# RMSNorm and SiLU on one core: transfers cut by partitions instead of by rows

## The chip, the core and the metric

The kernel runs on one core of one Trainium2 chip. The core has a buffer of 128 partitions, a vector engine (VectorE, DVE in the profile), an activation engine (ScalarE, ACT), a general engine (GpSimd, POOL), a matrix engine (TensorE, PE; here it does no arithmetic and only passes signals on), and a queue processor (SyncE, SP) that issues transfers. Sixteen DMA engines move data between the DRAM of the chip and the buffer. The metric is the device time of one execution in microseconds (us). The kernel before took 159.55 us as a median of three runs (159.41 to 160.32).

## The reference

The input `x` has 16 x 1024 rows of 512 float32 values. Each row is divided by its root mean square, multiplied by `gamma`, and put through the SiLU function:

```python
rms = np.sqrt(np.mean(x ** 2, axis=-1, keepdims=True) + eps)
x_norm = x / rms * gamma
return (x_norm * (1.0 / (1.0 + np.exp(-x_norm)))).astype(np.float32)
```

One row is 2 KB. All of `x` is 33.55 MB, the result as much, so 67.1 MB must pass through the DMA engines.

## The kernel before

**Tiles.** Every partition handles 128 rows (16,384 rows over 128 partitions). The buffer `xb` is a ring of 96 rows for each partition, 192 KB. Rows 0 to 95 of a partition have a place of their own in it; rows 96 to 127 go into the places of rows 0 to 31, once these are stored. All arithmetic is done in place, in units of `cn` = 4 rows (32 units).

**Rows in DRAM.** `groups` (L28) says which rows of DRAM belong to which rows of a partition. A group of g rows means that partition p owns g neighbouring rows of DRAM, so that a transfer of n of them is one unbroken piece of 2n KB for each partition. With groups of 16 a piece can be at most 32 KB, with groups of 32 it can be 64 KB. A piece of a partition is one packet of a DMA engine. A transfer over 128 partitions gives each of the sixteen engines eight packets.

**Transfers.** `loads` (L30 to L32) and `stores` (L33 to L35) list the transfers as (first row, rows); each covers all 128 partitions:

```python
    loads = [(0, 4), (4, 4), (8, 8), (16, 16), (32, 32), (64, 28), (92, 4)]
    loads += [(96, 16), (112, 12), (124, 4)]
    stores = [(0, 16), (16, 16)]
    stores += [(32, 32), (64, 32), (96, 16), (112, 8), (120, 8)]
```

`order` (L36 to L41) is the order by hand in which SP issues them, all on one queue: the seven loads of the first ring; a wait until load (64, 28) has landed; the two stores of rows 0 to 31 (the first middle phase); the three loads of rows 96 to 127 (the second middle phase); a wait until load (112, 12) has landed; the remaining stores. The first two loads are put ahead of the start barrier (`early`, L42). `load` (L127) lets SP wait for the stores whose places the load overwrites (L132): load (96, 16) waits for store (0, 16), load (112, 12) for store (16, 16). `store` (L138) waits until `s_swish` counts all units that hold its rows as done (L141). SP works in order: what waits holds up whatever stands behind it.

**Units.** For unit k, ACT squares the four rows (`square`, L205): two rows one by one with a sum (L207), two together into PSUM (L213); DVE sums the latter (`sums`, L232); POOL adds eps and takes the power -1/2 (`power`, L174); DVE multiplies each row by that and by gamma (`norm`, L241, L244); ACT applies SiLU (`swish`, L217, L219). ACT runs two units ahead with the squares (`lead`): after square k+2 comes swish k. Ten rounds of three units each run in a loop.

**Landings.** The first two squares wait for their loads themselves (L230). For all later units PE's queue waits for each load in turn (L168) and adds to `s_land` the number of units that are now complete; the square of a unit waits for that count.

## Time and profile before

| what | value |
|---|---|
| median of three runs | 159.55 us (159.41 to 160.32) |
| the profiled execution, its own time | 159.47 us |
| its span | 158.2 us |
| data moved | 67.12 MB, 424 GB/s over the span |
| ACT busy | 129.7 us (82%) |
| DVE busy | 124.5 us (79%) |
| POOL busy | 65.4 us (41%) |
| last SiLU ends | 143.8 us |

The span is the time between the first and the last instruction in the trace; the profiled execution's own time is 1.3 us longer. Busy times are sums over the whole span. The DMA rows of the page give the mean busy share of the sixteen engines; a queue's share is the time of its packets as a share of sixteen engines' span. The page lists no duration for a single packet, but the trace holds a record with start, duration and size for every packet; where such records are used they are called packet records.

### The profile page before, as it was taken

What the parts mean: (1) busy time and instruction counts of PE and PEld (TensorE: products, weight loads), DVE (VectorE), ACT (ScalarE), POOL (GpSimd) and SP (SyncE); (2) the same over time, 40 slices, a digit from 0 to 9 for tenths busy, and PEclk for the clock granted to TensorE, in tenths of its full rate; (3) what the DMA queues carried; (4) which work ended last, traced back from release to release, by engine and by line L of the source; (5) the groups of instructions that cost most, each with busy time, mean ns of one, the idle gap of its engine ahead of it and who ended that gap; (6) DMA issues with size and microseconds to landing.
All of it is one profiled execution on the core that took longest, in us unless ns stands there. A gap on an engine that the chain in (4) does not pass through costs nothing. (4 is left out here: it accounts for less than half of the span.)

```text
span 158.2 us, 696 instructions
## 1 busy us (share of the span) xinstructions
DVE 124.5 (79%) x162; ACT 129.7 (82%) x193; POOL 65.4 (41%) x70
## 2 busy tenths in 40 slices
DVE  0187968999199999999999999999999999980000
ACT  0949959996599999999999999999999999753000
POOL 1053555555055555555555555555555555510000
DMA  7999997979999879999999899996996998999896
GB/s 257 450 489 398 398 597 332 530 332 464 464 464 464 377 305 445 481 448 398 398 431 497 363 466 445 450 530 265 530 530 265 530 448 348 398 448 472 365 435 269
DMA packets 2456, 67.12 MB, mean 424 GB/s; under 512 B 276, under 2 KB 276, under 8 KB 280
## 3 DMA queue, kind: packets, MB, share of 16 engines
q1 hardware_dynamic: 2448, 67.11, 98.8%
q10 hardware_dynamic: 8, 0.01, 0.0%
HBM read 33.56 MB, written 33.55 MB: 424 GB/s over the span
## 5 line engine op out<-in xcount | busy, mean ns | idle before, releaser
L244 DVE SCALAR_TENSOR_TENSOR xb<-xb,rstd,gamma_sb 128x512 f32 (+1 forms) x128 | 87.3, 745 | 0.0
L219 ACT ACTIVATE xb<-xb (+1 forms) x32 | 60.9, 1903 | 2.8 <-DVE xb L244 2.8
L234 DVE TENSOR_REDUCE ms<-sq 128x2 f32<-128x1024 f32 x32 | 39.2, 1225 | 17.4 <-ACT sq L213 14.2
L177 POOL TENSOR_SCALAR aeps<-ms 128x4 f32<-128x4 f32 x32 | 20.6, 644 | 69.0 <-DVE ms L234 69.0
L184 POOL TENSOR_TENSOR rstd<-aeps,neg_half 128x4 f32<-128x4 f32 x32 | 44.1, 1378 | 2.7
L207 ACT ACTIVATE junk<-xb 128x512 f32 (+1 forms) x64 | 38.6, 603 | 7.8 <-PEq L168 7.5
L213 ACT ACTIVATE sq<-xb 128x1024 f32 (+1 forms) x32 | 32.2, 1005 | 0.0
L207 ACT ACTIVATION_READ_ACCUMULATOR junk<-xb 128x1 f32 x64 | 11.9, 186 | 0.0
L227 ACT ACT_TABLE_LOAD x1 | 1.3, 1283 | 3.6 <-issue 3.6
L170 POOL MEMSET gamma<- 128x512 f32 x1 | 0.5, 524 | 1.5 <-POOLq L75 1.5
L254 DVE STREAM_SHUFFLE gamma_sb<-gamma 128x512 f32<-128x512 f32 x1 | 0.7, 719 | 0.0
L319 POOL MEMSET const-float32-0.0<- 128x1 f32 x1 | 0.1, 98 | 0.2 <-issue 0.2
L171 POOL MEMSET neg_half<- 128x4 f32 x1 | 0.1, 102 | 0.0
L319 POOL MEMSET const-bfloat16-1.0<- 128x1 bf16 x1 | 0.1, 101 | 0.0
L319 POOL MEMSET const-uint8-127<- 128x1 uint8 x1 | 0.1, 101 | 0.0
L319 POOL MEMSET const-float32-1.0<- 128x1 f32 x1 | 0.1, 99 | 0.0
L254 DVE LOAD_MASK_SELECT gamma_sb<-gamma x1 | 0.0, 15 | 0.0
## 6 DMA issues: line engine op xcount, KB each, us to landing
out_dram<-xb SPq DMA_DIRECT2D x3, 4096.0 KB, 19.2
xb<-in_x_dram SPq DMA_DIRECT2D x2, 4096.0 KB, 19.5
xb<-in_x_dram SPq DMA_DIRECT2D x1, 7168.0 KB, 54.8
xb<-in_x_dram SPq DMA_DIRECT2D x4, 1024.0 KB, 12.9
out_dram<-xb SPq DMA_DIRECT2D x2, 2048.0 KB, 15.1
xb<-in_x_dram SPq DMA_DIRECT2D x1, 3072.0 KB, 16.8
xb<-in_x_dram SPq DMA_DIRECT2D x1, 2048.0 KB, 10.2
out_dram<-xb SPq DMA_DIRECT2D x2, 23.7
```

The costliest lines, as they stand in the source:

```text
L170: nc.gpsimd.memset(gamma4, 0.0).then_inc(s_zero, 1)
L171: nc.gpsimd.memset(neg_half, -0.5).then_inc(s_half, 1)
L177: nc.gpsimd.tensor_scalar(out=aeps[:, m, :], in0=ms[:, m, :], scalar1=eps_f, scalar2=None, op0=ALU.add,),
L184: nc.gpsimd.tensor_tensor(out=rstd[:, m, :], in0=aeps[:, m, :], in1=neg_half, op=ALU.pow),
L207: acc = nc.scalar.activation(out=junk[(k % turn) * (cn - n_sq) + j - n_sq], in_=rows(down(at, j), 1), func=AF.Square, scale=inv_d**0.5, ac ...
L213: nc.scalar.activation(out=sq[k % turn], in_=rows(at, n_sq), func=AF.Square, scale=inv_d**0.5,).then_inc(s_sq, 1)
L219: nc.scalar.activation(out=rows(at, cn), in_=rows(at, cn), func=AF.Silu),
L227: nc.scalar.preload_act_table_set("silu_and_others")
L234: nc.vector.tensor_reduce(out=ms[:, k % turn, 0:n_sq], in_=sq[k % turn], op=ALU.add, axis=mybir.AxisListType.X,),
L244: ins = nc.vector.scalar_tensor_tensor(out=one, in0=one, scalar=rstd[:, k % turn, j : j + 1], in1=gamma_sb, op0=ALU.mult, op1=ALU.mult,)
L254: nc.vector.stream_shuffle(gamma_sb, gamma4, [0] * 32), s_gld, 16
L319: nc = _bacc.Bacc("TRN2", target_bir_lowering=False, num_devices=1)
```

## The change

All groups have 32 rows. Each transfer has a third entry that says which partitions it covers: all (`every`), the even ones, the odd ones, or a part of the odd ones.

```diff
-    groups = [16, 16, 32, 32, 16, 16]
+    groups = [32, 32, 32, 32]
-    loads = [(0, 4), (4, 4), (8, 8), (16, 16), (32, 32), (64, 28), (92, 4)]
+    every, even, odd = (0, P), (0, P, 2), (1, P, 2)
+    loads = [
+        (0, 4, every),
+        (4, 12, every),
+        (16, 16, every),
+        (32, 32, every),
+        (64, 32, every),
+    ]
     second = len(loads)
-    loads += [(96, 16), (112, 12), (124, 4)]
-    stores = [(0, 16), (16, 16)]
+    loads += [
+        (96, 32, even),
+        (96, 32, (1, 128, 4)),
+        (96, 32, (3, 128, 8)),
+        (96, 32, (7, 128, 8)),
+    ]
+    stores = [(0, 32, even), (0, 32, odd)]
     storing = len(stores)
-    stores += [(32, 32), (64, 32), (96, 16), (112, 8), (120, 8)]
+    stores += [(32, 32, every), (64, 32, every), (96, 20, every), (116, 12, every)]
     order = [("load", i) for i in range(second)]
-    order += [("landed", loads.index((64, 28)))]
+    order += [("swished", 10)]
     order += [("store", t) for t in range(storing)]
     order += [("load", i) for i in range(second, len(loads))]
-    order += [("landed", loads.index((112, 12)))]
+    order += [("landed", 7)]
     order += [("store", t) for t in range(storing, len(stores))]
...
     def load(i):
-        a, n = loads[i]
-        for u, (c, m) in enumerate(stores):
+        a, n, p = loads[i]
+        for u, (c, m, q) in enumerate(stores):
             over = c + ring < a + n and a < c + m + ring
+            over = over and not set(range(*p)).isdisjoint(range(*q))
...
+        elif what == "swished":
+            nc.sync.wait_ge(s_swish, t)
...
+    passed = lead
+    for i in range(len(loads)):
+        landed = need(nc.tensor.nop(nofuse=True), ld[i], 16)
+        if landed_units[i] > passed:
+            landed.then_inc(s_land, landed_units[i] - passed)
+            passed = landed_units[i]
```

The even partitions of rows 0 to 31 are stored in one transfer of 64 partitions, the odd ones in a second. The even partitions of rows 96 to 127 are then loaded in one transfer (it waits for the even store), the odd ones in three: 32 partitions (1, 5, 9, ...), 16 partitions (3, 11, 19, ...) and 16 partitions (7, 15, 23, ...). The first of these three waits for the odd store. SP issues the first stores after ten units are through SiLU, where it waited for load (64, 28); it issues the later stores after the load of partitions 3, 11, ... has landed. A unit counts as landed once all 128 partitions of its rows are there (`landed_units`), so units 24 to 31 count only when the last of the four loads is complete. The last two stores have 20 and 12 rows, where three had 16, 8 and 8. Load (4, 12) takes the place of (4, 4) and (8, 8), and (64, 32) that of (64, 28) and (92, 4). The arithmetic and its order on ACT, DVE and POOL are the same.

More of the change, by code (lines that the diff above doesn't have):

```diff
@@ L52 @@
     for pieces in (loads, stores):
-        assert [a for a, _ in pieces] == [
-            sum(n for _, n in pieces[:i]) for i in range(len(pieces))
-        ]
-        assert sum(n for _, n in pieces) == rows_each
+        assert sum(n * len(range(*p)) for _, n, p in pieces) == rows_each * P
     K = rows_each // cn
@@ L61 @@
     per_ring = ring // (turn * cn)
-    landings, seen = [], 0
-    for k in range(K):
-        landings.append([])
-        while seen < len(loads) and loads[seen][0] < (k + 1) * cn:
-            landings[k].append(seen)
-            seen += 1
-    ends = [-(-(a + n) // cn) for a, n in stores]
+    landed_units, missing = [], {r: P for r in range(rows_each)}
+    for a, n, p in loads:
+        for r in range(a, a + n):
+            missing[r] -= len(range(*p))
+        landed_units.append(
+            next((r for r in range(rows_each) if missing[r]), rows_each) // cn
+        )
+    assert landed_units[-1] == K
+    ends = [-(-(a + n) // cn) for a, n, _ in stores]
     inv_d = 1.0 / float(D)
@@ L111, in dram @@
     def dram(ap, piece):
-        a, n = piece
+        a, n, p = piece
         g = max(g for g in range(len(groups)) if first[g] <= a)
@@ L116, in dram @@
         rows = ap[P * first[g] : P * (first[g] + groups[g])]
-        return rows.rearrange("(p n) d -> p n d", n=groups[g])[:, r : r + n, :]
+        return rows.rearrange("(p n) d -> p n d", n=groups[g])[slice(*p), r : r + n, :]
     def buf(piece):
-        a, n = piece
+        a, n, p = piece
         at = a % ring
         assert at + n <= ring, piece
-        return xb[:, at : at + n, :]
+        return xb[slice(*p), at : at + n, :]
     stored_by_sync = set()
     def load(i):
-        a, n = loads[i]
-        for u, (c, m) in enumerate(stores):
+        a, n, p = loads[i]
+        for u, (c, m, q) in enumerate(stores):
             over = c + ring < a + n and a < c + m + ring
+            over = over and not set(range(*p)).isdisjoint(range(*q))
             if over and u not in stored_by_sync:
@@ L163, in take @@
         need(queue.nop(nofuse=True), sem, n).then_inc(sem, -n)
-    for i, (a, n) in enumerate(loads):
-        units = (a + n) // cn - max(a // cn, lead)
-        if units > 0:
-            need(nc.tensor.nop(nofuse=True), ld[i], 16).then_inc(s_land, units)
+    passed = lead
[4 more added lines that the diff above has]
+            passed = landed_units[i]
     nc.gpsimd.memset(gamma4, 0.0).then_inc(s_zero, 1)
@@ L228 @@
     for k in range(lead):
-        assert landings[k] == [k]
-        square(k, k * cn, ld[k], 16)
+        by = next(i for i in range(len(loads)) if landed_units[i] > k)
+        assert by == k or landed_units[0] > k
+        square(k, k * cn, ld[by], 16)
     def sums(k, nth):
```

## The prediction

> **What bounds the kernel now.** I read the page's DMA rows first, because 67 MB for 158 us is a lot of traffic, then one stretch of the DMA view, then the chain and the waits of SP's queue.

> ```profile
> span 158.2 us, 696 instructions
> DMA  7999997979999879999999899996996998999896
> ...
> q1 hardware_dynamic: 2448, 67.11, 98.8%
> ...
> ACT 14%; DVE 4%; issue 2%; ACTq 0%
> ```

> The one queue with `x` and the result takes 98.8% of what sixteen DMA engines have in the span. The same view, narrowed to 60 to 80 us (the two first stores), leaves no gap at all:

> ```profile
> q1 hardware_dynamic: 298, 8.55, 100.0%
> ```

> By the packet records no engine is idle between 1.6 us and 156.7 us. What is lost is 1.0 us before the first packet, 0.2 us until all engines have started, about 0.6 us while they finish, and 0.5 us after them. The chain of the page covers only 20% of the span and ends with the last SiLU (141.92 + 1.91 = 143.8 us); from there the queue is alone. So the bound is the work in the DMA queue, and anything that lengthens a packet anywhere lengthens the end by as much, while a delay on ACT or DVE costs nothing until the queue runs empty. The reader can see in SP's waits that SP stands early:

> ```profile
> SPq L158 <- DMA xb<-in_x_dram: 69.7, 2, 53.8
> SPq L140 <- ACT xb L219: 45.2, 4, 15.7
> SPq L134 <- DMA out_dram<-xb: 20.9, 2, 11.3
> ```

> These waits are long, but each is over before the queue has worked off what was issued earlier.

> **Term 1: fewer, longer packets.** Median durations in the packet records are 309 ns for 8 KB, 611 for 16 KB, 912 for 24 KB, 1213 for 32 KB, 2116 for 56 KB and 2418 for 64 KB. That is a fixed 8 ns a packet (two of 32 KB less one of 64 KB: 2 x 1213 - 2418) and 27.2 bytes per ns and engine, for loads and stores alike. One engine's packets before are 32 of 8 KB, 24 of 16, 8 of 24, 40 of 32, 8 of 56 and 24 of 64, that is 136 packets and 155.33 us. After, they are 8 of 8 KB, 16 of 24, 8 of 32, 8 of 40 (not in the trace; 1514 ns on the line between 32 and 64 KB) and 48 of 64: 88 packets and 154.94 us. **The gain is 48 x 8 ns = 0.38 us.** This is all that 64 KB packets can bring. The packets' excess over their medians (0.5 us for each engine among the first 8 KB packets, 0.2 us near 78 us, where the first phase turns to loads) I leave as it is: both places are still there.

> **Term 2: the narrow transfers.** Every load and store of `x` before covers 128 partitions, so the trace shows no transfer of 64, 32 or 16. The bounds for one packet of such a transfer are 2418 ns (it runs as any 64 KB packet) and 4836 ns (two packets that must share what one has); below 2418 it can't go, as every size keeps to the same bytes per ns. The even, the odd and the (1, 128, 4) transfers take partitions out of every group of four neighbours equally: the same even load on all groups, with 4 or 2 packets for each engine. They are nearest to the 128-partition rows, and I take 2418, so nothing. The two transfers of 16 partitions are different: steps of 8 reach only every second group of four neighbours (3, 11, 19, ..., then 7, 15, 23, ...). Each engine has one packet in each. All sixteen engines then write to half of the groups, then to the other half. If the way into the buffer belongs to a group of partitions, engines meet two by two, and each of the two packets takes 4836 ns. Two rows speak to this. The four gamma packets (4 partitions, 2 KB, 84 ns each, at 6.3 to 7.2 us) ran beside full load traffic and no packet of `x` beside them is longer than its median; but they are 8 KB in all against 2 MB, which any small reserve on the way swallows. The first 8 KB packets of the kernel, which the engines begin nearly together, reach 1184 ns against 309, so packets can hold each other up. A steady 64 KB packet against another has no reserve; it is nearer to the second row, and I take the upper end, 2 x 2418 = **4.84 us**, with 0 as the other end.

> [...]

> **Term 3: what is late, and whether it is hidden: nothing.** Load (4, 12) lands where (8, 8) landed, so square 1 starts near 12.2 us (the unit after that load starts at 12.23) instead of 7.34. With the rows' 2.2 us for a square, 1.8 for a SiLU, 1.23 for a sum (L234) and 2.7 for four rows of `norm`, swish 5 then ends near 40.2 us instead of 38.0. ACT has room for that, as unit 8 waits for load (32, 32) anyway:

> ```profile
> 36.10 1.91 ACT L219 ACTIVATE xb<-xb  x1
> 41.29 0.63 ACT L207 ACTIVATE junk<-xb 128x512 f32 x1 [3.28 <-PEq L168]
> ...
> 55.46 1.91 ACT L219 ACTIVATE xb<-xb  x1
> ```

> The line at 55.46 us is the tenth SiLU. It ends at 57.37 us, and after the change SP issues the two first stores then; behind that wait stand all later transfers. Before, it issued them here, after load (64, 28) had landed at 57.65:

> ```profile
> 58.20 0.82 SPq L140 DMA_DIRECT2D out_dram<-xb  x2
> ```

> The first ring's loads keep the engines busy to about 60 us, and a transfer's first packet came 1.0 us after its issue (0.00 to 1.01). The queue runs dry only if the tenth SiLU ends after about 58.9 us, 1.5 us later than now; from there it costs one for one. The even load waits for the even store (landed near 70 us before for (0, 16)) while 9.7 us of odd store are queued, and the odd loads wait under 9.7 us of even load: covered, as now. The stores after "landed 7" have the last 1 MB load (2.4 us or more) as cover, as they have (124, 4) now. Units 24 to 31 must wait for the last load. It lands near 99.2 us before; with terms 1 and 2, near 103.7. Square 24 starts at 105.18 us, so there is 1 us left, and beyond that the SiLUs have more: store (96, 20) needs the 29th, at 133.2 us, and is due near 142; store (116, 12) needs the last, at 143.8, and is due near 154. SP's issues fall from 17 to 15, all under the queue.

> **The sum.** The profiled execution took 159.47 us: 159.47 - 0.38 + 4.84 = **163.9 us**. It lies 0.08 under the median of the runs, so the number stands for these too.

> **Rivals.**
> *No crowding*: the narrow transfers run like all others, and only term 1 is left: 159.47 - 0.38 = 159.1 us, no change that can be told, on the other side of my forecast. For it speak the gamma packets and that every large packet in the trace keeps to one rate; against it that no row has two engines with long packets on neighbouring partitions. It decides in one place, the stretch between 94 and 104 us. If the packets meet one after the other rather than sharing, one engine of a pair waits and the other runs on, and 1.2 to 2.4 us are lost: 160.3 to 161.5 us.
> *Crowding in all narrow transfers*: if the 64 and 32 partitions are also dealt out so that two engines meet, all 16 narrow packets of an engine double: 16 x 2418 ns = 38.7 us, 197.8 us. Against it is that these sets leave no group out; for it, that no row shows how 64 are dealt out.
> *A dry queue at the first turn*: the tenth SiLU is late by more than 1.5 us; every further us is added to the other cases. Against it are ACT's 3.28 us of idle time, of which I use 2.2.
> *That the change doesn't do what it says*, packets of 64 KB that are cut again, would cost back the 0.38 us only.

> **How the numbers follow.** Forecast with full crowding (162.5 to 165.3) 0.57; half of it (160.0 to 162.5) 0.08; none (158.8 to 160.0) 0.30; crowding everywhere or a dry queue (above 165.3) 0.05. The range from 158.9 to 165.3 takes in both ends of term 2 and leaves out the last case and the edges; the forecast's own range is 162.5 to 165.3. A measurement of this kernel can tell about 1% (1.6 us) from no change. Faster by over 1%: no term is that large, 0.01. Within 1% (to 161.1): no crowding and half of the half case, 0.34. Slower: 0.65.

> **What would show it.** The median 64 KB packet stays at 2418 ns in the even, odd and (1, 128, 4) transfers, and the 32 packets of the two 16-partition loads stand near 4.8 us. ACT's squares begin at 12.2 us and again near 41.3 us, the first stores are issued near 57.5 us, the queue has no gap, and the last SiLU still ends near 144 us. If those 32 packets are at 2.4 us, my term 2 is wrong and the time is 159.1; if the packets of the first stores are longer, the third case holds; if the queue is idle near 60 us, the fourth.

## The result, and the profile after

The changed kernel takes 164.84 us (median of six runs, 164.21 to 165.54) against 159.53 us for the kernel before on the same chips: 3.3% slower, ratio 1.033 with a 95% interval of 1.030 to 1.036. The forecast was 163.9. The profiled execution took 164.93 us with a span of 163.6, so its span is 5.4 us longer than before.

These are lines of the page of the changed kernel: span, the DMA busy share and the rate in forty slices of 4.1 us, the share of the one queue, and the chain that ended last.

```profile
span 163.6 us, 694 instructions
...
DMA  8999899599699989889699969999999999999894
GB/s 341 399 417 513 385 513 513 256 513 513 272 497 513 433 337 513 385 385 513 272 497 497 401 144 240 385 401 481 417 433 433 449 449 401 397 421 481 373 433 204
...
q1 hardware_dynamic: 1648, 67.11, 98.4%
...
ACT 14%; DVE 4%; issue 2%; ACTq 0%
```

The queue is as full as before (98.4% against 98.8%), with 800 fewer entries (each entry is a data packet or a signal of its landing). But one place stands out in the rate: 144 and 240 GB/s in the slices from 94 to 102 us, where the engines count as busy all the same. The same stretch by the view of stretches (busy time of DVE, ACT and POOL with instructions, clock, DMA share, GB/s):

```profile
94.70:102.70 8.00, 7.76 (x11) 8.00 (x13) 4.09 (x4) 1.00 0.67 147
105.00:141.00 36.00, 34.27 (x47) 33.30 (x49) 17.87 (x18) 1.00 1.00 435
```

The same stretch before:

```profile
94.70:102.70 8.00, 7.76 (x11) 8.00 (x13) 4.11 (x5) 1.00 1.08 464
```

A short stretch is rough here: the view counts a packet as a whole where it starts, and most packets of the first of the two loads start just ahead of 94.7 us, so 147 makes the drop look larger than it is. The durations are the safer measure. In these 8 us run the two loads of 16 partitions. By the packet records their 32 packets take 4.18 to 4.94 us each (median 4.79), while the median of all 768 packets of 64 KB is 2.42 as before.

The sum over the packet records, for each of the sixteen engines, says where the 5.4 us come from. The records name no engine, so "for each engine" is here and below the sum over all packets divided by sixteen; "excess" is time beyond the median duration of the packet's size.

| us for each engine | before | after | difference |
|---|---|---|---|
| packets at their median durations | 155.33 | 154.94 | -0.38 |
| excess of the 32 packets of the 16-partition loads | - | 4.54 | +4.54 |
| excess of other packets of 32 and 64 KB | 0.27 | 1.06 | +0.79 |
| excess of the 8 KB packets, nearly all of it among the first ones | 0.55 | 0.31 | -0.24 |
| engine idle, start and end included | 1.47 | 2.23 | +0.76 |

These add up to 5.47. Of the 1.06 us of other excess 0.2 lie at 57 us, where the first stores begin, 0.5 near 77 us, where these stores end and the loads begin, and 0.2 in the first packets of the later stores, from 102.7 us on. Of the idle time 1.2 us lie at the start in both. Some 0.6 of the 0.76 us of growth come from engines that finish less evenly: the last store's signals come from 156.78 to 157.64 us before, from 160.99 to 163.10 after.

SP's waits in the changed kernel, and ACT at the places that the prediction named:

```profile
SPq L172 <- ACT xb L235: 53.9, 1, 53.9
SPq L152 <- ACT xb L235: 41.4, 3, 19.6
SPq L146 <- DMA out_dram<-xb: 21.7, 2, 12.1
SPq L170 <- DMA xb<-in_x_dram: 19.4, 1, 19.4
```
```profile
11.86 0.63 ACT L223 ACTIVATE junk<-xb 128x512 f32<-128x512 f32 x1 [4.71 <-DMA xb<-in_x_dram]
...
41.02 0.63 ACT L223 ACTIVATE junk<-xb 128x512 f32 x1 [1.13 <-PEq L181]
...
55.18 1.91 ACT L235 ACTIVATE xb<-xb  x1
...
105.64 0.60 ACT L223 ACTIVATE junk<-xb 128x512 f32 x1 [0.65 <-PEq L181]
...
142.40 1.91 ACT L235 ACTIVATE xb<-xb 128x2048 f32<-128x2048 f32 x1 [0.74 <-DVE xb L261]
```

Square 1 waits for the longer second load; square 8 still waits for its load (1.13 us of the 3.28 us of idle time are left); the tenth SiLU ends at 57.1 us; square 24 waits 0.65 us for the last of the four loads; the last SiLU ends at 144.3 us, 19 us ahead of the end. None of this delays the queue: by the packet records sixteen packets or more are under way between 1.6 and 161 us, but for gaps of under 0.1 us and for 0.9 us near 80 us, with fifteen.

### The profile page after: what moved, and what is told of

Read it like the earlier page. It is cut to its first block, busy times and chain, and to the rows that moved or that the text cites. A ratio compares the mean times of both kernels' runs of the same rounds, so it can differ in the third digit from the quotient of the medians.

```text
span 163.6 us, 694 instructions
## 1 busy us (share of the span) xinstructions
DVE 124.5 (76%) x162; ACT 129.6 (79%) x193; POOL 65.4 (40%) x70
## 3 DMA queue, kind: packets, MB, share of 16 engines
q1 hardware_dynamic: 1648, 67.11, 98.4%
```

## The experiments

Four theories for the 4.8 us were put against each other. **A**: two engines meet where a transfer reaches only a part of the groups of partitions. **B**: a transfer with one packet for each engine is slow by itself. **C**: pieces 512 KB apart in DRAM are slow (16 partitions in steps of 8 are). **D**: all even and odd transfers are slow. All edits are made on the changed kernel unless said otherwise.

### One load of 32 partitions in place of two of 16

```diff
-        (96, 32, (3, 128, 8)),
-        (96, 32, (7, 128, 8)),
+        (96, 32, (3, 128, 4)),
...
-    order += [("landed", 7)]
+    order += [("landed", 6)]
```

> The two loads of 16 partitions become one of 32, (3, 128, 4), so every group of four neighbouring partitions is reached equally. Theory A (engines meet two by two where a transfer reaches only half of the groups): the 32 packets of 4.2 to 4.9 us go, every 64 KB packet is back near 2.42 us, and the time falls by the 4.6 to 4.8 us that they cost, to 160.0 to 160.3 us. If what is lost beyond that (164.84 measured against 163.9 forecast) comes from the crowding too, 159.1 to 159.5. Theory B (a transfer with one packet for each engine is slow by itself) and theory C (pieces 512 KB apart in DRAM are slow) expect the same here, since these go too. Theory D (the even and odd transfers are slow as well): stays above 162.

160.89 us, ratio to the kernel before 1.0078 (1.0063 to 1.0093). No packet is at 4.8 us any more, and theory D falls. But it is 0.6 us above what A allowed. The packet records show why: the last sixteen 64 KB packets of the second phase, which start at 96.3 to 97.5 us, take 3.03 to 3.84 us, 1.06 us for each engine over 2.42. They are the packets ahead of the turn from loads to stores.

### Two loads of 16 rows on 32 partitions

```diff
-        (96, 32, (3, 128, 8)),
-        (96, 32, (7, 128, 8)),
+        (96, 16, (3, 128, 4)),
+        (112, 16, (3, 128, 4)),
```

> The two loads of 16 partitions become two of 32 partitions, (3, 128, 4), with 16 rows each (two packets of 32 KB for each engine, 1 MB as before the last stores). Theories A, B and C: as with one load of 32 partitions, within 0.2 us of it, so 159.1 to 160.3. If the size of the last load before the stores matters, this one differs from that with a last load of 2 MB by more than 0.3 us.

159.84 us, ratio 1.0007 (0.9998 to 1.0016): the same partitions, the same 1 MB in the last load as in the changed kernel, and 5.0 us less than its 164.84. It differs from the kernel with one load of 32 partitions by 1.05 us, so something at the last load matters that none of the four theories had ("The turn from loads to stores" below finds it). The same stretch as above in this kernel:

```profile
94.70:102.70 8.00, 7.76 (x11) 8.00 (x13) 4.10 (x5) 1.00 1.08 467
```

All its 32 KB packets take 1.21 us, and all 64 KB packets of the even, odd and (1, 128, 4) transfers take 2.42 us but for those at the turn from stores to loads (0.6 us for each engine).

### Halves in place of even and odd

```diff
-    every, even, odd = (0, P), (0, P, 2), (1, P, 2)
+    every, even, odd = (0, P), (0, P // 2), (P // 2, P)
...
-        (96, 32, (1, 128, 4)),
-        (96, 32, (3, 128, 8)),
-        (96, 32, (7, 128, 8)),
+        (96, 32, odd),
...
-    order += [("landed", 7)]
+    order += [("landed", 5)]
```

> Even and odd become lower and upper half (partitions 0 to 63 and 64 to 127), in both middle phases; the upper half is loaded in one transfer. No transfer has 16 partitions; each engine has 4 packets of 64 KB in each. Theory A: each of these transfers reaches only half of the groups, so all 16 packets of an engine double, 16 x 2.42 = 38.7 us over some 160, so 199 us; if only writes into the buffer meet, not reads from it, the 8 of the loads, 179 us. Theory B: 160, since no transfer has one packet for each engine. Theory C: 160, since pieces are 64 KB apart.

200.83 us (one execution, as in the two runs below it). B and C had 160 here, so neither can be the whole account: 64 partitions with four packets for each engine and pieces next to each other in DRAM cost 5.1 us a packet (median) where the even 64 cost 2.42. That 5.1 is more than twice 2.42 is not explained. The two stores lose 9.8 and 9.5 us, the two loads 9.8 and 10.1 us, so here reads from the buffer lost as much as writes to it. The rate row of this kernel's page (slices of 5 us) shows the stretch of the four transfers, 60 to 140 us, at half the rate of what lies around it; below it the same by stretches:

```profile
GB/s 324 440 427 466 447 420 420 420 420 460 447 499 210 197 197 250 237 210 210 237 210 184 210 210 210 210 210 276 420 420 447 420 434 420 422 425 427 412 375 172
```
```profile
60.50:98.00 37.50, 36.44 (x49) 37.50 (x58) 19.68 (x20) 1.00 0.94 204
...
142.00:190.00 48.00, 33.62 (x44) 35.62 (x50) 16.36 (x16) 1.00 0.99 428
```

The first stretch lies in the two stores, at 204 GB/s over 37.5 us; in the second, transfers over all partitions run at 428 GB/s.

### Another two sets of 16 partitions

```diff
-        (96, 32, (3, 128, 8)),
-        (96, 32, (7, 128, 8)),
+        (96, 32, (3, 67, 4)),
+        (96, 32, (67, 128, 4)),
```

> The two loads of 16 partitions take other sets: 3, 7, ..., 63 and 67, 71, ..., 127. Pieces are then 256 KB apart in DRAM, as in the 128-partition transfers. Theory A: with the lower half of the partitions only half of the groups can be reached if the halves are what counts (the run with halves tells), and the loss stays, 164 to 165.5; if only the neighbourhood of four counts, all of 16 neighbourhoods have one packet each and the loss goes, 160. Theory B: 164 to 165.5. Theory C: 160.

164.81 us, as the changed kernel (164.84). 29 packets take over 4 us, in the same stretch:

```profile
94.50:103.00 8.50, 8.26 (x12) 8.50 (x14) 4.56 (x5) 1.00 0.74 170
```

Pieces are 256 KB apart in DRAM, as in the (1, 128, 4) transfer, whose packets take 2.42 us, so C falls a second time. The run below with one load of 32 partitions and later stores ("The turn from loads to stores") goes further: it moves the very same pieces, partitions 3, 7, ..., 127, in one transfer, and nearly all of its packets take 2.42 us. Only the cut into transfers differs.

The packet records tell against B too. In the changed kernel the first of the two loads has eight packets that start early, at 93.75 to 94.06 us; they take 4.18 to 4.55 us, and the eight that start at 94.38 to 96.06 us take 4.79 to 4.93. The last packet of the second load starts at 100.88 us, outlasts the others by 0.5 us and takes 4.21. In the kernel of this section the earliest packet, at 93.48 us, takes 3.34. These packets, which start before or end after the others of their load, are the shorter ones, and a load that is slow by itself would not show that. No run has a set of 16 partitions that goes at the full rate, which would be the direct test.

In this kernel sixteen neighbourhoods of four have one packet each, and 29 of the 32 packets take over 4 us all the same. So the prediction's "groups of four neighbours", an assumption of its author, are not what decides. Which partitions stand in each other's way the runs do not show; they show only which sets are slow. Packets of 64 KB are so over the lower and the upper half (5.1 us), over 16 partitions in steps of 8 (4.79 us), and over the two sets of this kernel; over all partitions, the even set and the (1, 128, 4) set they take 2.42 us.

### Four loads of 16 partitions

```diff
-        (96, 32, (1, 128, 4)),
+        (96, 32, (1, 128, 8)),
+        (96, 32, (5, 128, 8)),
...
-    order += [("landed", 7)]
+    order += [("landed", 8)]
```

> From the changed kernel, the load of 32 partitions (1, 128, 4) becomes two of 16, (1, 128, 8) and (5, 128, 8), so there are four loads of 16 partitions instead of two. Theory A: each costs 2.4 us, so 4.8 us more than the changed kernel's 164.84, 169.7 us, and 64 packets of about 4.8 us instead of 32. If crowding hides in part behind the engines' drift against each other, less than 4 us more.

169.29 us, 4.45 us over the changed kernel's median, and 64 packets over 4 us (median 4.83, excess 9.49 us for each engine against 4.54). The price is the same for each load, about 2.3 us.

### The turn from loads to stores

To the kernel with one load of 32 partitions at the end:

```diff
-    order += [("landed", 6)]
+    order += [("swished", 20)]
```

> As the run with one load of 32 partitions (3, 128, 4) at the end of the second phase (160.89 us), but SP issues the stores after 20 units are through SiLU (97.3 us in the trace) where it waited for the load before the last to land (issue at 95.4 us). Theory R (a transfer of the other direction that is in the queue early lengthens the last long packet ahead of it): the sixteen packets of 3.0 to 3.8 us that start at 96.3 to 97.5 us are back at 2.42 us and the time falls by 1.0 us, to 159.9. Theory S (the last 64 KB packet ahead of a change of direction is long in any case): 160.9, as before.

159.94 us against 160.89, ratio to before 1.0014 (1.0002 to 1.0025). Nothing but the moment of issue has changed. This is SP's timeline of both kernels between 90 and 100 us, first the one that waits for the load:

```profile
95.42 0.36 SPq L151 DMA_DIRECT2D out_dram<-xb  x1
```
```profile
97.27 0.35 SPq L151 DMA_DIRECT2D out_dram<-xb  x1
```

Issued at 95.42 us, the store lengthens the sixteen load packets that are under way from 96.3 us on by 1.06 us for each engine; issued at 97.27 us it lengthens them by 0.02. Theory R holds for this turn. The first turn fits it without an experiment of its own, as the moment of issue varies a little between the ten traces of kernels with 64 KB packets there. The last packets of load (64, 32) start at 57.0 to 57.8 us. Where the first store is issued at 57.18, 57.25 or 57.30 us, 9, 5 and 14 of the sixteen are lengthened; where it is issued at 57.34 to 57.61 us (seven traces), 0 to 2 are. The changed kernel, at 57.18, is the earliest. The number of long packets does not fall evenly with the moment of issue, so this is no more than a sign.

### The turn from stores to loads

To the kernel with two loads of 16 rows, to the one with a single load of 32 partitions and the later stores, and to the kernel before:

```diff
+    order += [("swished", 15)]
     order += [("load", i) for i in range(second, len(loads))]
```

> As the run with two loads of 16 rows on partitions (3, 128, 4) (159.84 us), but SP issues the loads of rows 96 to 127 only after 15 units are through SiLU (77.3 us in the trace), where it issued the first at 70.1 us. Theory R: the lengthening of the packets that start at 76.5 to 79.8 us (0.62 us for each engine) goes, to 159.2. Theory S: 159.8. If the issue now comes too late, the queue has a gap near 79 us and the time rises by that gap.

> Both edits on the kernel with one load of 32 partitions at the end. Theory R: 160.89 less 1.0 less 0.7 is 159.2, with all packets of 64 KB at 2.42 us in both middle phases. Theory S: 160.9. The gain of fewer packets alone (0.4 us) would then stand against the kernel before, whose median here is 159.6.

> The kernel before, with one edit: the loads of rows 96 to 127 are issued after 15 units are through SiLU. Theory R: the packets of 32 KB near 78 us (0.19 us for each engine over their median) shorten, to 159.4. Theory S: no change, 159.6.

In this order: 159.72 us, ratio 1.0011 (0.9998 to 1.0024); 159.77 us, 1.0013 (0.9999 to 1.0027); and 159.77 us, 1.0017 (1.0004 to 1.0031). SP issued the first of these loads at 77.28, 77.31 and 77.41 us, where the kernels without the edit did at 70.1 to 70.3, and the queue had no gap there of note (about 0.05 us for each engine; the kernel before also got one of 0.2 us for each engine near 99 us, where its later stores were issued at 98.59 instead of 97.19 us). But theory R falls here. In the first of the three nearly all of the odd store's last packets are back at 2.42 us, yet the load's first packets, from 78.95 us on, now take 2.75 to 3.61 us. The excess near the turn is 0.8 us for each engine, against 0.6 with the early issue, and in the kernel before it grows from 0.21 to 0.57. A later issue moves the loss to the other side of the turn.

### Short packets at that turn

To the kernel with two loads of 16 rows:

```diff
-        (96, 32, even),
+        (96, 4, even),
+        (100, 28, even),
...
-    stores = [(0, 32, even), (0, 32, odd)]
+    stores = [(0, 32, even), (0, 28, odd), (28, 4, odd)]
...
-    order += [("landed", 7)]
+    order += [("landed", 8)]
```

> From the run with two loads of 16 rows on partitions (3, 128, 4) (159.84 us): the odd store is cut in 28 and 4 rows, and the even load in 4 and 28, so that the packets on both sides of the turn from stores to loads have 8 KB instead of 64. Theory T (the turn lengthens whatever packets lie at it, in proportion to their size: 0.6 to 0.8 us for each engine with 64 KB, 0.2 with 32 KB in the kernel before): 0.1 us or less is left, and the time is 159.3 to 159.4. Theory U (the turn costs what it costs, with any packets): 159.8 to 159.9.

159.54 us, ratio 0.9995 (0.9981 to 1.0009). The time lies between the two forecasts and decides nothing; the records do. Packets of 8 KB at the turn take up to 0.68 us instead of 0.31, 0.52 us for each engine in all. Theory T falls; the loss is nearly that of 64 KB packets (0.62). Why it was only 0.2 us with the 32 KB packets of the kernel before stays open. This is the fastest of the variants with 64 KB packets, and it can't be told from the kernel before.

## Why the prediction was right, and where it was off

**What bounds the kernel** was right. Every run follows its packet records, and delays on ACT (0.65 us for square 24, 2 us for swish 5) show nowhere in the end.

**Term 1, fewer packets, -0.38 us**, is in the records (155.33 to 154.94 at median durations; the 40 KB packet that the trace lacked takes 1.514 us, as estimated), but no run got it as time. The sentence that failed is that the excess of the packets near 78 us would stay as it is. There the kernel before loses 0.2 us for each engine and the changed one 0.5. Without crowding, the packets of the kernel with two loads of 16 rows add up to 156.05 us for each engine against 156.17, and its time is that of before within 0.2%.

**Term 2, the narrow transfers, +4.84 us**, is what decided, and the upper end was the right one to take. That it was taken rested in part on luck: the row that the prediction held nearest, the first 8 KB packets at up to 1184 ns, belongs to loads over all 128 partitions, and no run shows that those packets are long for the same reason. The records show 4.54 us of excess, and taking the two loads away gains 5.0 us in time. The even, the odd and the (1, 128, 4) transfers cost nothing, as taken, and the rival that had them crowd as well falls with that; halves would have cost its 38.7 us (the halves' records have 39.1). The rival without crowding is refuted by the 32 packets at 4.8 us, and the gamma row that spoke for it was too small a test, 8 KB in all against 2 MB; that a small reserve on the way would take these was the author's assumption, and no run shows such a reserve. What the runs show is that packets of 64 KB take twice as long in transfers over some sets of partitions (4.79 us with 16 in steps of 8, 5.1 us with the halves, against 2.42 us), and not over others of the same number, such as the even 64. That engines meet there two by two is theory A's account of it; no record names the engine of a packet, so the meeting itself was not shown. The reason given for which partitions meet, groups of four neighbours, was an assumption, and it did not hold: in the run with sets 3, 7, ..., 63 and 67, 71, ..., 127 no such group has more than one packet of a load, and 29 of 32 packets take over 4 us.

**Term 3, cover**: right in that no delay reaches the queue, with the margins about as worked out but for one. Swish 5 ends at 39.9 us (40.2 forecast), the first stores are issued at 57.18 (57.5), the last SiLU ends at 144.3 (144). The exception is the load of units 24 to 31: it lands at 105.1 us instead of 103.7, which uses up the 1 us that was left, and square 24 waits 0.65 us, on time that ACT has to spare. What term 3 did not see are the packets lengthened by 0.2 us for each engine at 57 us, where the first stores are issued while the queue is full; that the early issue (57.18 us) is the cause has only the sign named above for it.

**The sum** is 0.9 us short of the 164.84 measured, and 1.0 us short of the profiled execution's 164.93. By the table above 0.8 us of packets lengthened where stores and loads take turns and 0.8 us of idle time, most of it from the uneven finish, are missing from it; term 2 was 0.3 too high and the 8 KB packets 0.2 better than assumed. That the sum came so near is in part errors that cancel.

## What to carry to other kernels

Before a transfer is cut by partitions, look at which partitions each part reaches, not at how many: here a packet of 64 KB took 2.42 us with the 64 even ones, as with all 128, 5.1 us with 64 neighbouring ones and 4.79 us with 16 in steps of 8; with 16 in steps of 4 within one half 29 of 32 took over 4 us. In this queue, 98.8% full before, 8 ns a packet was all that packets of 64 KB could save against two of 32 KB (2 x 1213 - 2418 ns), so compare that with what the cut may cost at turns between loads and stores. And a store issued 1.85 us too early (95.42 against 97.27 us), behind loads still under way, cost 0.95 us here (160.89 against 159.94 us), so the moment of issue is worth an experiment even where the queue never runs dry.
